# Softmax minus one-hot on one core: the middle blocks' transfers cut into four sets of every fourth partition, and the work ordered block by block

## The chip, the core and the metric

The kernel runs on one NeuronCore of one Trainium2 chip. A core has several engines that run side by side, each with its own instruction stream: VectorE (DVE in the profile), ScalarE (ACT), GpSimd (POOL), TensorE (PE) and SyncE (SP). Data moves between the device memory (HBM) and the core's on-chip memory (SBUF, 128 partitions) by DMA; the profile counts 16 DMA engines for the core. In this kernel SP and ACT issue the transfers, each into a queue of its own: the profile's q1 carries what SP issued, q10 what ACT issued.

The metric is the device time of one execution in microseconds (us). The kernel before takes 1248.91 us, the median of three runs (1248.84 to 1249.3).

## The reference

For 8 x 1024 rows of 8192 logits, the gradient of a cross entropy: the softmax of the row, less 1 at the label's column. All in fp32.

```python
logits_max = np.max(logits, axis=-1, keepdims=True)
exp_logits = np.exp(logits - logits_max)
softmax = exp_logits / np.sum(exp_logits, axis=-1, keepdims=True)
one_hot = np.zeros_like(logits)
one_hot[batch_idx, seq_idx, labels] = 1.0
return (softmax - one_hot).astype(np.float32)
```

Input and output are 268.4 MB each. Every element has to come in once and go out once.

## The kernel before

**Tiling.** The 8192 rows are cut into 32 blocks of 256 rows. In a block, partition p holds rows 2p and 2p+1 (G = 2 rows for each partition), so both in memory and in SBUF a partition's share of a block is one contiguous run of 64 KB, 32 KB for each of its two rows. A block is 8.39 MB. The big buffer `X` has three slots (SLOTS = 3); block b lives in slot b mod 3 and is computed in place: loaded, exponentiated, scaled, stored. A "row tile" t = 2b + j is one of the two rows of all 128 partitions, 128 x 8192 elements. There are 64 of them.

**Per row tile.** Four steps, each a helper of the code:

- `row_max(t)`: a VectorE reduction over the row gives the negated maximum `m`. It waits for the pieces of the load that meet this row.
- `exponentials(t)`: ScalarE's Exp in place, which also accumulates the sum `s`.
- `mark(t)`: two short ScalarE instructions on 128 x 2048 elements that write the one-hot row into PSUM (`hot`, one buffer for even and one for odd row tiles), as bytes. It may start when the row tile two before has been finished.
- `finish(t)`: on VectorE a reciprocal of `s`, and one pass X = X * r - hot in place. For the last two row tiles the pass is made in two halves of the columns.

**Transfers.** `load(b)` and `store(t)` cut a block into pieces by a letter for each block, in the strings LOADS and STORES: `r` is one transfer for each of the two rows, 128 partitions with runs of 32 KB; `s` is row by row in two sets of every second partition, 64 runs of 32 KB each, of which the second set goes by ACT's queue; `w` is the whole block in one transfer, 128 runs of 64 KB. Loads go by SP's queue, stores by ACT's. A load of block b + 3 waits for all the stores of block b that share partitions and rows with it, because it overwrites their slot. A store of a row waits for its `finish`. In the kernel before, blocks 0 to 2 are loaded as `s`, 3 and 4 as `r`, 5 to 28 as `w`, 29 to 31 as `r`, and all stores are `r`; the last block is stored in four transfers, one for each row and half of the columns.

**Order.** The string ORDER sets by a letter how the instructions of a block are put in line on VectorE and ScalarE. In the kernel before it is `r` throughout: the code interleaves, and the reduction of the next block's first row stands ahead of the finish of this block's second row. On VectorE, with t the first row tile of a block: row_max(t+1), finish(t), row_max(t+2), finish(t+1), row_max(t+3), finish(t+2) and so on. With `b` a block is done by itself: row_max(t), row_max(t+1), finish(t), finish(t+1), and only then the next block. The branch for `b` is in the code of the kernel before, unused. Stores and loads are issued from the same program order: a store of a row after its finish, the load of block b + 3 after both stores of block b.

**The helper.** All instructions go through `run`, so that in the profile nearly everything stands at its line, L76; a wait for more than one semaphore is a wait of its own at L75 ahead of the instruction. So the profile is read here by operation and by tile names.

Of the kernel before, what the change touches and what calls it, by code (L numbers as in the profile page):

```python
# [7 lines left out]
P = 128  # L8
G = 2
SLOTS = 3  # L10

LOADS = "sssrrwwwwwwwwwwwwwwwwwwwwwwwwrrr"
STORES = "rrrrrrrrrrrrrrrrrrrrrrrrrrrrrrrr"
ORDER = "rrrrrrrrrrrrrrrrrrrrrrrrrrrrrrrr"


@with_exitstack
def kernel(
# [45 lines left out]
    with tc.tile_critical():  # L64
# [6 lines left out]
        def run(engine, waits, counter, method, **operands):  # L71

            waits = list(dict.fromkeys(waits))
            for w in waits[:-1]:
                engine.wait_ge(*w)  # L75
            instruction = getattr(engine, method)(**operands)  # L76
            for w in waits[-1:]:
                instruction._wait_ge(*w)
            step = 16 if method == "dma_start" else 1
            instruction.then_inc(counter, step)  # L80
            count[counter.name] = count.get(counter.name, 0) + step
            return counter, count[counter.name]

        every, rows = slice(0, P), slice(0, G)
        one = [slice(j, j + 1) for j in range(G)]
        halves = [slice(i, P, 2) for i in range(2)]
        sides = [slice(i * V // 2, (i + 1) * V // 2) for i in range(2)]
        PIECES = {
            "r": [(every, js) for js in one],
            "s": [(ps, js) for js in one for ps in halves],  # L90
            "w": [(every, rows)],
        }

        def meets(a, b):
            sets = [[set(range(*d.indices(n))) for d, n in zip(p, (P, G))] for p in (a, b)]
            return all(x & y for x, y in zip(*sets))
# [4 lines left out]
        def load(b):  # L101
            loaded[b] = []
            before = stored.get(b - SLOTS, [])
            for q, piece in enumerate(PIECES[LOADS[b]]):
                ps, js = piece
                free = [w for other, w in before if meets(piece, other)]
                queue = nc.scalar if LOADS[b] == "s" and ps == halves[1] else nc.sync
                w = run(
# [5 lines left out]
        def store(t):  # L114
            b, j = divmod(t, G)
            stored.setdefault(b, [])
            if t >= T - G:
# [6 lines left out]
                return  # L124
            for q, piece in enumerate(PIECES[STORES[b]]):
                ps, js = piece
# [30 lines left out]
        def mark(t):  # L157
            if t >= T:
                return
            w = run(  # L160
                nc.scalar, ([made] if t < G else [freed[t - G]]) + ([marked[t - 1]] if t else []), act, "activation",
                out=away[:], in_=count16[:], func=Act.Abs, bias=at(word, t), scale=1.0,
            )
            marked[t] = run(
                nc.scalar, [w], act, "activation",
                out=hot[:, t % G, :], in_=away[:], func=Act.Relu, bias=at(unit, t), scale=at(minus, t),
            )
# [76 lines left out]
        for b in range(B):  # L244
            t0, t1 = b * G, b * G + 1
            nxt = t1 + 1
            if ORDER[b] == "b":
                if t0 not in maxed:
# [20 lines left out]
            mark(t0 + G)  # L269
            ahead = nxt < T and ORDER[b + 1] == "r"  # L270
            if ahead:
# [41 lines left out]
```

## Time and profile before

| what | value |
|---|---|
| time, median of 3 runs | 1248.91 us |
| span of the profiled execution, first to last instruction | 1246.6 us |
| VectorE busy | 1120.2 us (90%) |
| ScalarE busy | 722.7 us (58%) |
| DMA busy, mean of 16 engines, over all but the two ends | 1.00 |
| moved | 536.98 MB, mean 431 GB/s |

The profiled execution's own time was not given apart from its span; the median of the runs lies 2.3 us above the span, and what lies around the span (launch and end) is taken to be that. How to read it: a line of the page's last part and of the views by group gives the engine, the operation, output and input, and a count; "q1" and "q10" rows count the DMA packets. A packet here is one contiguous run of a transfer (a run of 32 KB or 64 KB), or the small completion message that each of the 16 engines sends at the end of a transfer.

### The profile page before, as it was taken

The numbers are of one execution on the slowest core, as the hardware profiler recorded it, in microseconds if no ns is written. First come the engines' busy times: TensorE is split into PE (matmuls) and PEld (weight loads), VectorE is DVE, ScalarE is ACT, GpSimd is POOL, SyncE is SP. The second block draws the span as 40 slices with busy tenths as digits, with TensorE's granted clock in tenths as the row PEclk, the third lists the DMA queues.
The fourth block names the chain that finished last, engine by engine and source line by source line (L and its number), as shares of the span: only waits on it lengthen the run. The fifth ranks groups of instructions, "written<-read, shape, count | busy, mean of one in ns | idle before, by whom it ended". The sixth has DMA issues, their size and how long they took to land.

```text
span 1246.6 us, 809 instructions
## 1 busy us (share of the span) xinstructions
PE 0.4 (0%) x2; PEld 0.3 (0%) x2; DVE 1120.2 (90%) x208; ACT 722.7 (58%) x257; POOL 2.3 (0%) x7
## 2 busy tenths in 40 slices
PE   0000000000000000000000000000000000000000
PEld 0000000000000000000000000000000000000000
DVE  5999998889988889888898888998889988899995
ACT  2866664556555565465655655556556555566662
POOL 0000000000000000000000000000000000000000
DMA  9999999999999999999999999999999999999998
GB/s 406 413 431 434 437 432 444 435 437 421 433 429 437 443 423 433 434 431 435 430 441 435 422 435 435 434 440 426 432 434 431 433 446 434 422 430 435 429 434 383
DMA packets 15413, 536.98 MB, mean 431 GB/s; under 512 B 1808, under 2 KB 1808, under 8 KB 1840
## 3 DMA queue, kind: packets, MB, share of 16 engines
q10 hardware_dynamic: 9744, 276.89, 51.5%
q1 hardware_dynamic: 5664, 260.05, 48.3%
q14 instruction: 5, 0.04, 0.0%
HBM read 268.50 MB, written 268.44 MB: 431 GB/s over the span
## 4 chain that ended last, share of the span: by engine, by line
DMA 59%; DVE 26%; issue 11%; ACT 3%; DVEq 0%; ACTq 0%; SPq 0%
DMA X<-in_logits_dram 33%; DMA out_dram<-X 26%; DVE X L76 15%; DVE m L76 10%; ACT X L76 2%; DVEq L64 0%; DVE r L76 0%; ACT hot L76 0%; ACT away L76 0%; ACTq L76 0%; DVEq L75 0%; ACTq L308 0%; SPq L64 0%
## 5 line engine op out<-in xcount | busy, mean ns | idle before, releaser
L76 ACT ACTIVATE X<-X,m 128x8192 f32<-128x8192 f32 x64 | 455.8, 7122 | 365.2 <-DVE m L76 365.2
L76 DVE TENSOR_REDUCE m<-X 128x1 f32<-128x8192 f32 x64 | 555.6, 8682 | 105.4 <-DMA X<-in_logits_dram 105.4
L76 DVE SCALAR_TENSOR_TENSOR X<-X,r,hot 128x8192 f32<-128x8192 f32 (+1 forms) x66 | 560.1, 8489 | 3.8 <-ACT hot L76 1.6
L76 ACT ACTIVATE away<-count,word 128x2048 bf16<-128x2048 int16 x64 | 128.1, 2001 | 127.0 <-DVE X L76 127.0
L76 ACT ACTIVATE hot<-away,unit,minus 128x2048 int32<-128x2048 bf16 x64 | 131.9, 2061 | 2.1
L76 ACT ACTIVATION_READ_ACCUMULATOR X<-X,m 128x1 f32 x64 | 11.9, 186 | 0.0
L76 DVE RECIPROCAL r<-s 128x1 f32<-128x1 f32 x64 | 9.8, 153 | 0.0
L76 ACT ACT_TABLE_LOAD x1 | 1.3, 1283 | 5.3 <-issue 5.3
L76 DVE CAST lab_f<-lab_raw 32x256 f32<-32x256 int32 x1 | 0.5, 536 | 2.7 <-DMA lab_raw<-in_labels_dram 2.7
L76 POOL IOTA count<- 128x2048 int16 x1 | 1.8, 1823 | 0.0
L76 DVE TENSOR_TENSOR unit<-unit,part 128x64 f32<-128x64 f32 x3 | 0.7, 225 | 0.1
L76 DVE CAST lab<-hot 128x64 int32<-128x64 f32 x1 | 0.2, 224 | 0.5 <-PE hot L76 0.5
L76 DVE TENSOR_SCALAR part<-minus 128x64 f32<-128x64 f32 x3 | 0.6, 194 | 0.1
L76 PE MATMUL hot<-ident,lab_f 32*128 32x32 f32 x2 | 0.4, 298 | 3.3 <-DVE lab_f L76 3.3
L76 PEld LDWEIGHTS hot<-ident,lab_f 32*128 32x128 f32 x2 | 0.3, 192 | 3.3 <-DVE lab_f L76 3.3
L76 DVE CAST minus<-lab 128x64 f32<-128x64 int32 x1 | 0.2, 195 | 0.0
L76 DVE TENSOR_SCALAR word<-part 128x64 f32<-128x64 int32 x1 | 0.2, 195 | 0.0
L76 DVE TENSOR_SCALAR lab<-lab 128x64 int32<-128x64 int32 x1 | 0.2, 195 | 0.0
L76 DVE TENSOR_SCALAR unit<-minus 128x64 f32<-128x64 f32 x1 | 0.2, 195 | 0.0
L76 DVE TENSOR_SCALAR part<-lab 128x64 int32<-128x64 int32 x1 | 0.2, 194 | 0.0
L76 DVE TENSOR_SCALAR minus<-unit 128x64 f32<-128x64 f32 x1 | 0.2, 194 | 0.0
L76 POOL TENSOR_SCALAR_AFFINE_SELECT ident<-ident 32x32 f32<-32x32 f32 x1 | 0.2, 203 | 0.1
(5 smaller groups left out, 0.5 us busy)
## 6 DMA issues: line engine op xcount, KB each, us to landing
out_dram<-X ACTq DMA_DIRECT2D x62, 4096.0 KB, 30.4
X<-in_logits_dram SPq DMA_DIRECT2D x10, 4096.0 KB, 28.1
X<-in_logits_dram SPq DMA_DIRECT2D x6, 2048.0 KB, 32.6
X<-in_logits_dram ACTq DMA_DIRECT2D x6, 2048.0 KB, 37.1
out_dram<-X SPq DMA_DIRECT2D x2, 2048.0 KB, 12.7
out_dram<-X ACTq DMA_DIRECT2D x2, 2048.0 KB, 11.9
X<-in_logits_dram SPq DMA_DIRECT2D x24, 33.4
lab_raw<-in_labels_dram ACTq DMA_DIRECT2D x1, 64.0 KB, 1.8
```

What stands on the lines that cost most here:

```text
L76: instruction = getattr(engine, method)(**operands)
```

## The change

Three strings and one new letter. The new letter `q` cuts a block into four sets of every fourth partition, each with both rows: 32 runs of 64 KB, 2.1 MB. Loads of blocks 5 to 28 become `q` where they were `w`. Stores of blocks 2 to 25 become `q` where they were `r`; since a `q` piece holds both rows, all four are issued after the finish of the block's second row. ORDER is `b` throughout. A load of block b + 3 is now cut as the store of block b is, so each of its four pieces waits for one piece of the store.

```diff
-LOADS = "sssrrwwwwwwwwwwwwwwwwwwwwwwwwrrr"
-STORES = "rrrrrrrrrrrrrrrrrrrrrrrrrrrrrrrr"
-ORDER = "rrrrrrrrrrrrrrrrrrrrrrrrrrrrrrrr"
+LOADS = "sssrrqqqqqqqqqqqqqqqqqqqqqqqqrrr"
+STORES = "rrqqqqqqqqqqqqqqqqqqqqqqqqrrrrrr"
+ORDER = "bbbbbbbbbbbbbbbbbbbbbbbbbbbbbbbb"
...
+        fourths = [slice(i, P, 4) for i in range(4)]
...
             "w": [(every, rows)],
+            "q": [(ps, rows) for ps in fourths],
         }
```

The number of transfers goes from 113 to 233: loads from 46 to 118 (24 whole blocks become 96 sets), stores from 66 to 114 (48 rows become 96 sets), and one for the labels.

## The prediction

> **What bounds the kernel now.** I read first the page's busy rows, its slices and its DMA rows.
>
> ```profile
> span 1246.6 us, 809 instructions
> PE 0.4 (0%) x2; PEld 0.3 (0%) x2; DVE 1120.2 (90%) x208; ACT 722.7 (58%) x257; POOL 2.3 (0%) x7
> DMA  9999999999999999999999999999999999999998
> DMA packets 15413, 536.98 MB, mean 431 GB/s; under 512 B 1808, under 2 KB 1808, under 8 KB 1840
> q10 hardware_dynamic: 9744, 276.89, 51.5%
> q1 hardware_dynamic: 5664, 260.05, 48.3%
> ```
>
> VectorE at 90% looks like the bound at first. But the two DMA queues together hold 51.5 + 48.3 = 99.8% of all the time of 16 engines. So I read the waits and a stretch of the chain next, and then the stages by window.
>
> ```profile
> DVE m L76 <- DMA X<-in_logits_dram: 105.4, 26, 8.9
> ...
> 637.14 26.24 DMA out_dram<-X
> 663.38 0.02 issue
> 663.40 33.30 DMA X<-in_logits_dram
> ```
>
> ```profile
> core 0: us, PE busy (x) PEld busy (x) DVE busy (x) ACT busy (x) POOL busy (x), PEclk, DMA share, GB/s
> 10.00:50.00 40.00, 0.00 (x0) 0.00 (x0) 31.66 (x5) 25.40 (x10) 0.00 (x0) 1.00 1.00 433
> 50.00:62.00 12.00, 0.00 (x0) 0.00 (x0) 11.96 (x4) 8.14 (x3) 0.00 (x0) 1.00 1.00 399
> 165.00:1080.00 915.00, 0.00 (x0) 0.00 (x0) 821.48 (x142) 530.10 (x189) 0.00 (x0) 1.00 1.00 433
> 1080.00:1200.00 120.00, 0.00 (x0) 0.00 (x0) 116.13 (x22) 74.01 (x27) 0.00 (x0) 1.00 0.99 428
> ```
>
> VectorE's waits for data (105.4 us in 26) are the larger part of its idle time. The chain shows why: a store of 26 us, a load of 33 us in the slot that it freed, then compute. That looks like a chain of latencies, which finer pieces would shorten. The windows say that it isn't: from 10 us on the DMA share is 1.00 at 433 GB/s, in the middle as at the start. The store and the load last long because they share full engines. Shortening a wait then only moves the same bytes in another order. The bound is bytes over 16 engines, plus what each packet costs beside its bytes.
>
> So the questions are three: does the change alter what the packets cost, does it leave the engines without work anywhere, and does a set of 32 partitions move as fast as 128.
>
> **The packets.** Three short windows show what one packet takes; in each row stand packets, MB and the share of 16 engines. The first holds one completion message, the second row tiles' stores alone, the third has loads of whole blocks on q1.
>
> ```profile
> DMA packets 1, 0.00 MB, mean 0 GB/s; under 512 B 1, under 2 KB 1, under 8 KB 1
> q10 hardware_dynamic: 1, 0.00, 0.6%
> ...
> DMA packets 256, 7.34 MB, mean 432 GB/s; under 512 B 32, under 2 KB 32, under 8 KB 32
> q10 hardware_dynamic: 256, 7.34, 100.0%
> ...
> DMA packets 138, 6.09 MB, mean 435 GB/s; under 512 B 16, under 2 KB 16, under 8 KB 16
> q1 hardware_dynamic: 64, 4.19, 69.1%
> ```
>
> The first window is 0.1 us long (1244.9 to 1245): 0.6% of 16 x 0.1 us is 0.0096 us for a message. The second is 17 us long (1202 to 1219): 272.0 us of engine time, less 32 messages (0.31 us), over 224 runs of 32 KB gives 1.2129 us each. The third is 14 us long (638 to 652): 69.1% of 224 us over 64 runs of 64 KB (4.19 MB over 64 is 65.5 KB, so q1 holds no message there) gives 2.4185 us. Two runs of 32 KB take 2.4258 us, so joining them saves 0.0073 us. With the shares' rounding (0.05% each) that is 0.004 to 0.010 us.
>
> *Removed.* Loads of blocks 5 to 28 are in runs of 64 KB already and stay so; "transfers of 64 KB runs" is new for the stores alone. There 24 blocks x 128 partitions = 3072 pairs of runs become one, 192 on each engine: 192 x 0.0073 = 1.40 us (0.8 to 2.0).
>
> *Added.* 1808 small packets are 16 for each of 113 transfers; 233 transfers have 3728. That is 1920 more, 120 on each engine: 120 x 0.0096 = 1.15 us if each takes the engine for itself, 0 if it hides beside a run of the other queue. I take 1.15, since the row shows that time.
>
> *Bytes*: the same. So the DMA's work changes by 1.15 - 1.40 = -0.25 us, between -2.0 and +0.35.
>
> **Issuing, and the engines.**
>
> ```profile
> L76 ACTq DMA_DIRECT2D out_dram<-X x64: 337/338/373, 44.6 to 1233.1; - x64
> L76 SPq DMA_DIRECT2D X<-in_logits_dram x40: 327/328/657, 1.0 to 1173.0; - x40
> L76 ACT ACTIVATE X<-X,m 128x8192 f32<-128x8192 f32 x64 | 455.8, 7122 | 365.2 <-DVE m L76 365.2
> L76 ACT ACTIVATE hot<-away,unit,minus 128x2048 int32<-128x2048 bf16 x64 | 131.9, 2061 | 2.1
> L76 ACT ACTIVATE away<-count,word 128x2048 bf16<-128x2048 int16 x64 | 128.1, 2001 | 127.0 <-DVE X L76 127.0
> 1101.76 8.68 DVE L76 TENSOR_REDUCE m<-X 128x1 f32<-128x8192 f32 x1
> 1110.36 0.15 DVE L76 RECIPROCAL r<-s 128x1 f32<-128x1 f32 x1
> 1110.54 8.75 DVE L76 SCALAR_TENSOR_TENSOR X<-X,r,hot 128x8192 f32<-128x8192 f32 x1
> 1119.21 8.68 DVE L76 TENSOR_REDUCE m<-X 128x1 f32<-128x8192 f32 x1
> ```
>
> VectorE needs 1119.21 - 1101.76 = 17.45 us for a row tile, 34.9 for a block. The DMA needs 2 x 8.39 MB / 433 GB/s = 38.75 us. In the new order, finish(t) stands behind row_max(t+1) (8.68 us), and the Exp that it needs takes 7.12 + 0.19: hidden. The second Exp hides behind finish(t) (8.75). On ScalarE four issues of 0.34 (1.35 us, before 0.68) and a mark (2.0 + 2.06) come after the block's last finish, 5.4 us in all; the next Exp can start only after the next block's first reduction, 8.68 us later. So the added issues are behind that, at nothing; without this cover 0.68 us of ScalarE a block, still below the slack of 3.85 us that VectorE has. Of the waits that the change moves, the four stores on ACT's queue wait for the block's second finish, and behind them stand that mark and the next Exp, for which VectorE asks last; on SP's queue a set waits for its own store, and behind it stands only the next set, whose store ends later. SP has nothing else to do but issue, 96 x 0.33 us. VectorE's extra waits, six a block, are for semaphores that have come by then or come with the last piece; the row shows gaps of a few hundredths of a us between instructions, so 0.3 us a block at most, in the same slack.
>
> **Do the engines run dry?** A middle block's store now starts when its second row is finished: for the first row 8.9 us later. Take the moment a block b is finished: its slot has 8.39 MB to store, and 8.39 MB of load queue behind it set by set. That is 38.75 us of DMA work, and VectorE hands over the next block 34.9 us later at the earliest. If instead VectorE stands still for data, a load is in flight by definition. So the middle stays full. A set's load waits for its store to land, but three other sets (4.8 us each at full rate) are in the ring meanwhile.
>
> The first place at risk is block 2, the first stored in sets. From the timeline's start of the first reduction at 15.75 us the new order finishes block 0 at 56 us, block 1 at 91 and block 2 at about 126 (44.5 us for the first finish, then from 47.1, when the second Exp is done, one pass, and two blocks of 34.9). Until then five loads and two stored blocks, 58.7 MB, can move; at the 423 GB/s of the first 155 us they last 139 us. A margin of 12 us.
>
> ```profile
> 15.75 8.69 DVE L76 TENSOR_REDUCE m<-X 128x1 f32<-128x8192 f32 x1 [8.91 <-DMA X<-in_logits_dram]
> 35.78 8.75 DVE L76 SCALAR_TENSOR_TENSOR X<-X,r,hot 128x8192 f32<-128x8192 f32 x1 [1.56 <-ACT hot L76]
> 39.74 7.11 ACT L76 ACTIVATE X<-X,m 128x8192 f32<-128x8192 f32 x1
> 0.00:155.00 155.00, 0.41 (x2) 0.28 (x2) 139.63 (x37) 95.27 (x35) 2.31 (x7) 1.00 0.99 423
> ```
>
> At the end, the window from 1202 has no q1 packet: stores alone for the last 43 us. When the last load lands, at most a reduction and two finishes are left on VectorE (8.68 + 2 x 8.9 = 26.5 us) and a last store of 11.9 us to landing (below); 38.4 in all, against two whole blocks to store, 38.75 us. Covered, by the old margin or little less.
>
> ```profile
> out_dram<-X ACTq DMA_DIRECT2D x2, 2048.0 KB, 11.9
> lab_raw<-in_labels_dram ACTq DMA_DIRECT2D x1, 64.0 KB, 1.8
> ```
>
> **Sum.** 1246.6 - 0.25 = 1246.35 us of span, and the 2.3 us by which the median stands above it: 1248.6 us. Own range 1246.9 to 1249.3. VectorE will wait less or elsewhere, and that is worth nothing.
>
> **Rivals.**
>
> *The hand-over hole (slower).* A set's load starts only when its set is stored, and a store lands some time after its last byte; the label's small load took 1.8 us in all. If the other ring is empty at that moment, once a block, 24 x 1.8 = 43 us are lost: 1292. It decides as soon as less than 1.8 us of work stands in the rings. For it: all stores of a block start together, so the two rings can fall into step. Against: 38.75 against 34.9 us. 10%.
>
> *The sets move slower (slower).* Two runs for each engine instead of eight may not spread as evenly, and the page has no set of 32 partitions. The nearest rows are the sets of 64 at the start, 433 GB/s between 10 and 50 us, which is no loss, and, as the other end, 428 between 1080 and 1200: 402.7 MB in sets at 428 instead of 433 is 10.9 us, 1259.5. 5%.
>
> *A fixed price for each transfer (slower).* 120 transfers more, each with the label's 1.8 us on the path, is 216 us: 1465. Against it: stores alone keep the engines at 100.0% over 17 us in which two transfers ended (32 messages). 3%. [...]
>
> *Faster.* The fixed cost of a run at its upper bound (2.0 us), messages for nothing, and the slow stretch at 50 to 62 us (399 instead of 433 GB/s, 0.94 us) gone: 1246.6 - 2.94 + 2.3 = 1246.0. Against: the stretch belongs to blocks 0 to 2, cut as before. 5%.
>
> **How the numbers follow.** The forecast holds 77%, all of it within 0.2% (2.5 us, what a measurement can tell from no change here). Faster 5%, slower 10 + 5 + 3 = 18%. The range starts at 1246.5, below the forecast's lower bound, and reaches to 1254, half of the second rival, which leaves out 2 in 10.
>
> **What would show it.** Small packets 3728 and some 10,500 runs; queue shares that still sum to 99.8%; 433 or 434 GB/s in the middle; chain pieces that name other transfers while the span stays. Wrong would be: slices of DMA under 9 after the start (the hole), a full share at fewer GB/s (slower sets), or VectorE without waits for loads (then it, not the DMA, is the bound).

## The result, and the profile after

The changed kernel takes 1252.2 us, the median of 5 runs (1251.07 to 1255.52); the kernel before, on the same chip, takes 1248.84 (1248.18 to 1249.3). The ratio is 1.0034, with the 95% interval from 1.0021 to 1.0047: it is 3.4 us slower. The profiled execution took 1254.47 us, of which the span is 1252.7; it is one of the longer ones, so what its trace shows is more than the 3.4 us of the medians. Medians below are of all runs and ratios of the undisturbed ones alone, and for two experiments only a median is left.

The page of the changed kernel, the rows that answer to those of before:

```profile
span 1252.7 us, 1001 instructions
PE 0.4 (0%) x2; PEld 0.3 (0%) x2; DVE 1120.3 (89%) x208; ACT 722.8 (58%) x257; POOL 2.3 (0%) x7
DMA  9999999999999999999999999999999999999997
DMA packets 14264, 537.02 MB, mean 429 GB/s; under 512 B 3728, under 2 KB 3728, under 8 KB 3760
q10 hardware_dynamic: 7440, 276.90, 51.3%
q1 hardware_dynamic: 6816, 260.05, 48.3%
```

The engines compute as long as before, and no slice before the last has lost its 9. The small packets are the 3728 that were counted ahead. The two queues together hold 99.6% instead of 99.8% of the 16 engines' time, at 429 GB/s instead of 431. So there is a little more idle time, and the busy time moves less.

VectorE's wait for loads, and a stretch of the chain that ended last (start, duration, what):

```profile
DVE m L76 <- DMA X<-in_logits_dram: 104.3, 27, 9.0
```

```profile
626.80 45.29 DMA out_dram<-X
672.11 33.56 DMA X<-in_logits_dram
705.83 8.47 issue
714.30 7.40 DVE m L76
```

VectorE still stands 104 us for data (105.4 before). The chain names longer pieces, a store of 45 us where it was 26, and yet in that part of the program nothing is lost: these lengths are queueing in front of full engines (a share of 1.00 at 434 GB/s from 345 to 1070 us, below). Where the loss is, only the rate by stretches of time shows. First the windows of the kernel before (window, length, busy time of each engine, clock, DMA share, GB/s), then those of the changed one. A run is counted whole in the window in which it begins, so a short window can show a share above 1.00; its rate divided by its share is then the rate of full engines:

```profile
10.00:137.00 127.00, 0.00 (x0) 0.00 (x0) 118.48 (x20) 82.71 (x30) 0.00 (x0) 1.00 1.00 430
137.00:152.00 15.00, 0.00 (x0) 0.00 (x0) 14.96 (x4) 9.49 (x4) 0.00 (x0) 1.00 1.04 448
152.00:345.00 193.00, 0.00 (x0) 0.00 (x0) 171.71 (x30) 111.32 (x40) 0.00 (x0) 1.00 1.00 433
345.00:1070.00 725.00, 0.00 (x0) 0.00 (x0) 652.77 (x112) 420.51 (x150) 0.00 (x0) 1.00 1.00 434
1070.00:1105.00 35.00, 0.00 (x0) 0.00 (x0) 31.30 (x7) 21.14 (x8) 0.00 (x0) 1.00 0.98 421
1105.00:1235.00 130.00, 0.00 (x0) 0.00 (x0) 127.81 (x25) 76.29 (x27) 0.00 (x0) 1.00 1.00 432
1240.00:1245.00 5.00, 0.00 (x0) 0.00 (x0) 0.00 (x0) 0.00 (x0) 0.00 (x0) 1.00 0.68 292
1245.00:1250.00 5.00, 0.00 (x0) 0.00 (x0) 0.00 (x0) 0.00 (x0) 0.00 (x0) 1.00 0.00 2
```

```profile
10.00:137.00 127.00, 0.00 (x0) 0.00 (x0) 115.90 (x20) 78.01 (x29) 0.00 (x0) 1.00 1.00 429
137.00:152.00 15.00, 0.00 (x0) 0.00 (x0) 14.93 (x4) 11.93 (x5) 0.00 (x0) 1.00 1.01 415
152.00:345.00 193.00, 0.00 (x0) 0.00 (x0) 174.49 (x30) 112.78 (x41) 0.00 (x0) 1.00 1.00 430
345.00:1070.00 725.00, 0.00 (x0) 0.00 (x0) 653.49 (x111) 421.33 (x150) 0.00 (x0) 1.00 1.00 434
1070.00:1105.00 35.00, 0.00 (x0) 0.00 (x0) 34.93 (x7) 22.55 (x8) 0.00 (x0) 1.00 0.99 416
1105.00:1235.00 130.00, 0.00 (x0) 0.00 (x0) 123.48 (x25) 74.88 (x26) 0.00 (x0) 1.00 1.00 431
1240.00:1245.00 5.00, 0.00 (x0) 0.00 (x0) 0.00 (x0) 0.00 (x0) 0.00 (x0) 1.00 0.93 397
1245.00:1250.00 5.00, 0.00 (x0) 0.00 (x0) 0.00 (x0) 0.00 (x0) 0.00 (x0) 1.00 0.37 157
```

Three things stand there.

- From 345 to 1070 us both kernels move 434 GB/s. A steady state of sets costs neither more nor less than one of whole loads and row stores.
- From 137 to 345 us and again from 1070 to 1105 the changed kernel moves less at a full share. These are the changes from rows to sets and back, called passages here: block 2, the first stored as a set, is finished at 126 us, and at 1070 to 1105 the cuts go back to rows. Rate over share gives 448 / 1.04 = 431 before and 415 / 1.01 = 411 after from 137 to 152 us, and 430 and 420 from 1070 to 1105. The rates' differences times the windows' lengths give, from 10 to 1235 us, 0.13 + 0.50 + 0.58 + 0 + 0.18 + 0.13 = 1.5 MB, which is 3.5 us at 433 GB/s (the rounding of the long window alone is worth over 1 us). The records of the single runs agree: a run of 32 KB nearly always takes 1.213 us and one of 64 KB 2.418, and what the runs took above that adds up, for each engine, to about 5.6 us in the changed kernel and 2.5 in the one before. From 137 to 345 us it is 2.6 against 0.1, from 1070 to 1105 1.1 against 0.0, and between these two 0.1 against 0.8. A run that took longer than usual is called a stretched run from here on.
- After 1240 us the engines have 0.93 x 5 + 0.37 x 5 = 6.5 us of work each, where they had 3.4. That is the 3.1 us again. But it is spread unevenly: between 1245 and 1250 more and more engines are idle while some still work. Of the 6.1 us by which the profiled span grew, about 3.1 are stretched runs and the rest is this spread. The last engine ends this kernel, not the mean of 16: from 1245 to 1250 us that mean is 0.37.

The changed kernel's first passage, 137 to 152 us, read out (all packets, then the load queue's: packets, MB, share of 16 engines):

```profile
DMA packets 149, 6.23 MB, mean 415 GB/s; under 512 B 20, under 2 KB 20, under 8 KB 20
q1 hardware_dynamic: 68, 2.23, 39.0%
```

The 68 load packets are runs of 32 KB (2.23 MB over 68), of blocks that are still loaded by rows of 128 partitions. They take 39.0% of 240 us over 68 = 1.38 us each instead of 1.21. So at a passage it isn't the runs of the sets alone that are stretched.

### The profile page after: what moved, and what is told of

It reads as the page before. It is cut to its first block, busy times and chain, and to the rows that moved or that the text cites. A ratio compares the mean times of both kernels' runs of the same rounds, so it can differ in the third digit from the quotient of the medians.

```text
span 1252.7 us, 1001 instructions
## 1 busy us (share of the span) xinstructions
PE 0.4 (0%) x2; PEld 0.3 (0%) x2; DVE 1120.3 (89%) x208; ACT 722.8 (58%) x257; POOL 2.3 (0%) x7
## 2 busy tenths in 40 slices
DMA packets 14264, 537.02 MB, mean 429 GB/s; under 512 B 3728, under 2 KB 3728, under 8 KB 3760
## 4 chain that ended last, share of the span: by engine, by line
DMA 57%; DVE 25%; issue 11%; ACT 2%; another core or an unknown queue 2%; ACTq 1%; DVEq 0%; SPq 0%
DMA out_dram<-X 33%; DMA X<-in_logits_dram 25%; DVE X L76 14%; DVE m L76 11%; ACTq L76 1%; ACT X L76 1%; DVE r L76 0%; DVEq L64 0%; ACT hot L76 0%; ACT away L76 0%; DVEq L75 0%; SPq L76 0%; ACTq L310 0%; ACTq L75 0%
## 5 line engine op out<-in xcount | busy, mean ns | idle before, releaser
L76 DVE TENSOR_REDUCE m<-X 128x1 f32<-128x8192 f32 x64 | 553.1, 8680 | 104.3 <-DMA X<-in_logits_dram 104.3
```

## Experiments

All diffs are against the changed kernel, and `b` order is kept unless the diff says otherwise. The kernel before took 1248.25 to 1248.58 us on the same chips. The letters of theories hold within one group of runs; the text beside a letter says what it holds.

### The order alone, and the cut alone

```diff
 e1_order_only
-LOADS = "sssrrqqqqqqqqqqqqqqqqqqqqqqqqrrr"
-STORES = "rrqqqqqqqqqqqqqqqqqqqqqqqqrrrrrr"
+LOADS = "sssrrwwwwwwwwwwwwwwwwwwwwwwwwrrr"
+STORES = "rrrrrrrrrrrrrrrrrrrrrrrrrrrrrrrr"
 e2_sets_only
-ORDER = "bbbbbbbbbbbbbbbbbbbbbbbbbbbbbbbb"
+ORDER = "rrrrrrrrrrrrrrrrrrrrrrrrrrrrrrrr"
```

> Only ORDER is b; the transfers are cut as before. Theory S (the sets of 32 partitions put the 16 engines out of step and slow runs where the cut changes): 1248.8 us, ratio 0.999 to 1.001, the last store's 16 completions within 3 us of each other as before. Rival O (the order by block costs it): 1251.5 to 1253. Rival L (runs of 64 KB in both directions at once cost it): 1248.8, as S.

> The middle blocks in sets of every fourth partition both ways, ORDER r as before. Theory S: 1251.5 to 1253, ratio about 1.003, engines 7 us or so apart at the end. Rival O: 1248.8. Rival L: 1251.5 to 1253, as S.

Measured: the order alone 1248.58 us, ratio 1.0001 [0.9992, 1.0009]; the sets in the old order 1270.37, 1.0166 [1.0143, 1.0190]. The order costs nothing by itself, and with the sets it saves 18 us; that was in none of the forecasts for the second run. Without it the stretched runs are 25.9 us an engine, 22.9 of them in the 64 KB loads, and they go on through the whole middle, where the load queue runs empty 62 times (in the changed kernel once between 165 and 1070 us; gaps of over 0.3 us without a load run are counted).

### Other cuts in both directions

```diff
 e3_whole_both
+LOADS = "sssrrwwwwwwwwwwwwwwwwwwwwwwwwrrr"
+STORES = "rrwwwwwwwwwwwwwwwwwwwwwwwwrrrrrr"
 e4_halves_both
+LOADS = "sssrrhhhhhhhhhhhhhhhhhhhhhhhhrrr"
+STORES = "rrhhhhhhhhhhhhhhhhhhhhhhhhrrrrrr"
+            "h": [(ps, rows) for ps in halves],
 e9_rows_both
+LOADS = "sssrrrrrrrrrrrrrrrrrrrrrrrrrrrrr"
+STORES = "rrrrrrrrrrrrrrrrrrrrrrrrrrrrrrrr"
```

> Middle blocks move whole both ways, one transfer of 128 runs of 64 KB each way, ORDER b: the runs of the changed kernel without its sets. Theory S: 1247 to 1249 us, no slower than before, engines within 3 us at the end. Rival L: 1251.5 to 1253, as the changed kernel. Rival O: 1251.5 to 1253.

> Middle blocks in two sets of every second partition, both rows, runs of 64 KB, ORDER b: four runs for each engine in a transfer instead of two (sets) or eight (whole). Theory S with the number of runs for each engine as its cause: between, 1249 to 1251. Rival L: 1251.5 to 1253.

> All middle blocks row by row both ways, runs of 32 KB only, ORDER b. Theory L: no slow runs; 1248.8 us plus 192 runs more for each engine at 0.0073 us (1.4), so 1250. If mixing run lengths is what keeps before undisturbed: slower than 1252.

Measured: whole blocks 1290.59 us, 1.0323 [1.0297, 1.0348]; two sets of every second partition 1258.82, 1.0081 [1.0049, 1.0113]; rows 1248.57, 1.0001 [0.9992, 1.0010]. The first two lie outside every forecast.

The slices of the page of the kernel with whole blocks, and its window over the middle and over one hole, show what the prediction called the hand-over hole:

```profile
DMA  9999999999989999999999999999999999999998
```

```profile
165.00:1070.00 905.00, 0.00 (x0) 0.00 (x0) 774.16 (x134) 498.13 (x178) 0.00 (x0) 1.00 0.98 413
358.00:361.00 3.00, 0.00 (x0) 0.00 (x0) 2.71 (x1) 0.00 (x0) 0.00 (x0) 1.00 0.05 22
```

The load of a slot must wait for the whole block's store there, and the engines run out of work: one slice in the middle falls below 9, and the share of 0.98 over 905 us is 18 us of holes. In the hole at 358 to 361 us the share is 0.05 at 22 GB/s, the work of about one engine of 16. But the loss is 42 us. The rest is again at a full share: runs are stretched, many of them right after such a hole, by 29.6 us an engine in all. So this isn't a matter of sets of 32 partitions alone; whole transfers of 128 have it too.

Rows in both directions leave all runs at 32 KB, and the time is that of before. This bears on the other half of the prediction's sum, the prices of joined runs and of messages. The same window, 400 to 1000 us, of the kernel before, of the changed one and of rows both ways:

```profile
DMA packets 6658, 259.65 MB, mean 433 GB/s; under 512 B 736, under 2 KB 736, under 8 KB 736
```

```profile
DMA packets 5956, 260.09 MB, mean 433 GB/s; under 512 B 1984, under 2 KB 1984, under 8 KB 1984
```

```profile
DMA packets 8926, 259.91 MB, mean 433 GB/s; under 512 B 992, under 2 KB 992, under 8 KB 992
```

From 3972 to 7934 runs, and from 736 to 1984 messages, move the same within 0.44 MB, 1 us of 600. The prices forecast for this window are smaller than that (about 0.4 us saved and 0.75 us added for an engine, by the prediction's 0.0073 and 0.0096 us), so these windows neither confirm nor refute them. They do show that the two prices aren't the loss.

### Sets in one direction alone

```diff
 e6_stores_sets
+LOADS = "sssrrwwwwwwwwwwwwwwwwwwwwwwwwrrr"
 e7_loads_sets
+STORES = "rrrrrrrrrrrrrrrrrrrrrrrrrrrrrrrr"
 e10_set_rows
+STORES = "rrpppppppppppppppppppppppprrrrrr"
+            "p": [(ps, js) for js in one for ps in fourths],
 (and eight semaphores for each slot instead of four)
 e16_halves_loads
+LOADS = "sssrrhhhhhhhhhhhhhhhhhhhhhhhhrrr"
+STORES = "rrrrrrrrrrrrrrrrrrrrrrrrrrrrrrrr"
```

> Loads whole as before, stores of the middle blocks in sets of every fourth partition with runs of 64 KB, ORDER b. Theory L (runs of 64 KB in both directions at once slow some runs, loads above all): slower, 1251 to 1290 us, slow load runs in the middle. Theory S (sets of 32 partitions): 1250 to 1252. If sets soften what whole transfers do, it lies between the changed kernel (1252) and the whole both ways (1290).

> Loads of the middle blocks in sets with runs of 64 KB, stores row by row with runs of 32 KB, ORDER b. Theory L: 1248 to 1249.5 us, the middle without slow runs as before. Theory S: 1250.5 to 1253.

> The changed kernel with its middle stores cut once more, by row: eight sets of 32 runs of 32 KB instead of four of 64 KB; loads in sets of 64 KB runs, ORDER b. Theory L: no slow runs, 1249.5 to 1251 us (1.4 for the runs, 0.9 for 96 completion messages more on each engine), engines together at the end. Theory S: 1252 to 1254, engines 7 us apart at the end.

> Loads in two sets of every second partition with runs of 64 KB (four runs for each engine in a transfer), stores by rows, ORDER b: between whole loads beside stores by rows (1248.6, eight runs) and loads in four sets beside them (1280.7, two runs). If the few runs of a set for each engine cost at each restart of the load queue: 1255 to 1270. If every cut into sets does: 1275 to 1285.

Measured: sets for stores alone 1298.1 us, 1.0397 [1.0382, 1.0413]; sets for loads alone 1280.73, 1.0255 [1.0235, 1.0275]; loads in sets with stores in eight sets of 32 KB runs 1278.33, 1.0242 [1.0225, 1.0259]; halves for loads alone 1252.61, 1.0036 [1.0023, 1.0049]. So sets of every fourth partition in one direction cost 32 to 50 us, in both with the stores cut by rows as well 30, and in both, cut alike, 3.4. For halves it is the other way round: 4 us in loads alone, which is below both forecasts, and 10 in both. Theory L is refuted, since the loads in sets lose as much beside 32 KB stores; theory S has the sign, but its sizes are far too small. With sets for stores alone a whole load has to wait for all four sets of its slot, and the window from 165 to 1070 us shows a share of 0.99 at 413 GB/s: small holes and stretched runs, as with whole blocks.

The kernel with sets for loads alone shows stretched runs at their plainest. At 243.5 us its load queue starts again after 7 us of stores alone. Its window from 243 to 250 us (packets and MB, then q1's packets, MB and share of 16 engines):

```profile
DMA packets 51, 2.72 MB, mean 389 GB/s; under 512 B 0, under 2 KB 0, under 8 KB 0
q1 hardware_dynamic: 32, 2.10, 79.2%
```

And the order alone, from 241 to 248 us, where the load queue starts again with a whole block after 10 us of stores alone:

```profile
DMA packets 61, 3.05 MB, mean 435 GB/s; under 512 B 0, under 2 KB 0, under 8 KB 0
q1 hardware_dynamic: 32, 2.10, 69.4%
```

Both hold 32 load runs of 64 KB, two for each engine. They take 79.2% of 112 us over 32 = 2.77 us each in the first and 2.43 in the second, and the stores beside them move less as well: 0.33 MB lost in 7 us, 0.8 us. This comes back with every block, 0.9 us on the mean; with the order alone the same restart costs 0.05 us on the mean, with halves 0.05.

### Sets from the first block to the last, and 32 neighbours

```diff
 e5_sets_throughout
+LOADS = "qqqqqqqqqqqqqqqqqqqqqqqqqqqqqqqq"
+STORES = "qqqqqqqqqqqqqqqqqqqqqqqqqqqqqqqr"
 e8_quarters
+LOADS = "kkkkkkkkkkkkkkkkkkkkkkkkkkkkkkkk"
+STORES = "kkkkkkkkkkkkkkkkkkkkkkkkkkkkkkkr"
+            "k": [(slice(32 * i, 32 * i + 32), rows) for i in range(4)],
```

> All blocks in sets both ways from the first load on (only the last block's stores stay cut by rows), ORDER b: no change of cut at 126 us and at 1075 us. Theory R (a set's runs are slow when its queue starts again after running empty, because 16 engines start in step and collide until they have drifted apart; once apart they stay so while the queue never empties): slow runs in the first load-only stretch, few later; 1248 to 1252 us. Theory C (the changes of cut are what costs): 1247.5 to 1249.

> As the sets throughout, but a set is a quarter of 32 neighbouring partitions instead of every fourth. [...] If only the size of the transfer and the restart decide: within 1% of the sets throughout.

Measured: sets throughout 1261.76 us, 1.0099 [1.0074, 1.0125], slower than either theory had it; 32 neighbouring partitions 1682.55 us. Windows of the first:

```profile
55.00:66.00 11.00, 0.00 (x0) 0.00 (x0) 11.00 (x2) 3.37 (x2) 0.00 (x0) 1.00 0.67 286
165.00:1070.00 905.00, 0.00 (x0) 0.00 (x0) 821.83 (x141) 529.68 (x188) 0.00 (x0) 1.00 1.00 433
1245.00:1255.00 10.00, 0.00 (x0) 0.00 (x0) 0.00 (x0) 0.00 (x0) 0.00 (x0) 1.00 0.74 318
```

With no passage in the middle, it is at the full rate again. It pays at its ends: a hole of 0.33 x 11 = 3.6 us around the first stores, and engines that end apart. So doing away with passages by cutting everything into sets is no way out.

How the 32 partitions are chosen matters more than anything else here. In the window from 10 to 50 us there are loads almost alone. First every fourth partition, then neighbours:

```profile
DMA packets 400, 17.83 MB, mean 446 GB/s; under 512 B 128, under 2 KB 128, under 8 KB 128
q1 hardware_dynamic: 400, 17.83, 102.9%
```

```profile
DMA packets 224, 8.42 MB, mean 211 GB/s; under 512 B 80, under 2 KB 80, under 8 KB 96
q1 hardware_dynamic: 192, 8.39, 101.6%
```

The second moves 128 runs of 64 KB in 101.6% of 640 us: 5.1 us each against 2.42. So the loads of 32 neighbours move at half the rate, 211 GB/s, where every fourth partition takes the full rate (446 at a share of 1.029). Stores pay less: by the page of the kernel with neighbours, q10 moves 264.31 MB in 39.9% of 16 engines' span of 1687.7 us, 2.67 us for each 64 KB. The size of the transfer and the restart alone would have left the time within 1% of the sets throughout; it is 33% longer. What makes neighbours slow is not shown.

### What keeps the changed kernel near 1252: each set waits only for its own piece

```diff
 e12_drain
-                free = [w for other, w in before if meets(piece, other)]
+                free = [w for _, w in before]
```

> The changed kernel with one thing undone: each of the four load sets waits for all four store sets of its slot instead of for its own, so that the load queue runs empty once a block; cuts and order stay. Theory R: slow load runs once a block, 1262 to 1295 us, as the order r with sets (1270) and sets in one direction alone (1281, 1298). Theory M (unlike cuts of the two directions, or the order r, were what cost there): 1251 to 1255, as the changed kernel.

The edit holds for every load of a block whose slot has been stored, the loads by rows included.

Measured: 1305.46 us, 1.0484 [1.0428, 1.0540], more than theory R had. Its window over the middle:

```profile
165.00:1070.00 905.00, 0.00 (x0) 0.00 (x0) 771.67 (x133) 500.19 (x178) 0.00 (x0) 1.00 0.98 411
```

Share 0.98 instead of 1.00 is 18 us of holes, and the stretched runs of the whole program are 35 us an engine. The 53 us above the changed kernel are what the waits by pieces are worth.

### The passages counted: twelve blocks in sets, in one, two and four stretches

```diff
 e13_one_change
+LOADS = "sssrrqqqqqqqqqqqqrrrrrrrrrrrrrrr"
+STORES = "rrqqqqqqqqqqqqrrrrrrrrrrrrrrrrrr"
 e14_two_changes
+LOADS = "sssrrqqqqqqrrrrrrqqqqqqrrrrrrrrr"
+STORES = "rrqqqqqqrrrrrrqqqqqqrrrrrrrrrrrr"
 e15_four_changes
+LOADS = "sssrrqqqrrrqqqrrrqqqrrrqqqrrrrrr"
+STORES = "rrqqqrrrqqqrrrqqqrrrqqqrrrrrrrrr"
```

> The changed kernel with half as many blocks in sets: 12 blocks in sets, then rows both ways, ORDER b; one stretch of sets as in the changed kernel. Theory C (what is lost is lost at the passages between rows and sets, one into the stretch and one out of it): 1251.5 to 1253 us, as the changed kernel. Theory P (lost evenly over the blocks in sets): 1250 to 1250.8, half the loss.

> The same 12 blocks in sets, in two stretches of six with six blocks in rows between them. Theory C: twice the loss of one stretch, 1255 to 1257 us. Theory P: as with one stretch, 1250 to 1250.8.

> The same 12 blocks in sets, in four stretches of three. Theory C: four times the loss, 1260 to 1265 us. Theory P: 1250 to 1250.8.

Measured: one stretch 1253.49 us, 1.0063 [1.0038, 1.0089]; two 1292.59 (single runs from 1268.54 to 1303.99); four 1305.02, 1.0459 [1.0432, 1.0486]. Half the blocks in sets, in one stretch, cost as much as all of them, and half of them in four stretches cost 57 us. So the loss doesn't go by the number of blocks, which refutes theory P. It grows with the number of passages, but with two and four stretches it is about six and four times what theory C had. The windows of the kernel with one stretch, whose sets end near 600 us, show it:

```profile
125.00:175.00 50.00, 0.00 (x0) 0.00 (x0) 49.93 (x9) 32.29 (x11) 0.00 (x0) 1.00 1.02 434
175.00:590.00 415.00, 0.00 (x0) 0.00 (x0) 374.38 (x66) 242.44 (x88) 0.00 (x0) 1.00 1.00 433
590.00:640.00 50.00, 0.00 (x0) 0.00 (x0) 49.68 (x10) 31.93 (x11) 0.00 (x0) 1.00 0.99 414
640.00:1070.00 430.00, 0.00 (x0) 0.00 (x0) 393.13 (x69) 255.15 (x91) 0.00 (x0) 1.00 1.00 433
```

The passage back, which was at 1070 us, has moved to 590 to 640: 414 instead of 433 GB/s over 50 us, about 2 us. On both sides of it the rate is full. In the first stretch the load queue stands empty for about 1 us at every set, at no cost: from 175 to 590 us the share is 1.00 at 433 GB/s all the same. With two and four stretches the rate doesn't stay full any more. Of the kernel with two, its second stretch of sets and the rows behind it; then, of the kernel with four, the two long windows:

```profile
600.00:900.00 300.00, 0.00 (x0) 0.00 (x0) 227.00 (x40) 144.23 (x54) 0.00 (x0) 1.00 0.94 391
920.00:1200.00 280.00, 0.00 (x0) 0.00 (x0) 260.02 (x44) 166.01 (x60) 0.00 (x0) 1.00 1.00 431
```

```profile
175.00:590.00 415.00, 0.00 (x0) 0.00 (x0) 370.62 (x66) 238.40 (x86) 0.00 (x0) 1.00 1.00 419
640.00:1070.00 430.00, 0.00 (x0) 0.00 (x0) 351.70 (x61) 221.10 (x79) 0.00 (x0) 1.00 0.96 401
```

The price of a passage isn't fixed. After a later one the runs stay stretched and holes come (shares 0.94 and 0.96) for as long as the stretch of sets lasts, and they end with the return to rows. Why the one long stretch keeps the full rate and a later one doesn't is not shown.

### Why the runs are stretched: addresses, bytes of a run, or runs for each engine

```diff
 e17_sets_in_line, e18_loads_in_line
+        def place(letter, q, ps):
+            return slice(32 * q, 32 * q + 32) if letter == "q" else ps
...
-                    out=X[ps, b % SLOTS, js, :], in_=x_b[b, ps, js, :],
+                    out=X[ps, b % SLOTS, js, :], in_=x_b[b, place(LOADS[b], q, ps), js, :],
...
-                    out=o_b[b, ps, js, :], in_=X[ps, b % SLOTS, js, :],
+                    out=o_b[b, place(STORES[b], q, ps), js, :], in_=X[ps, b % SLOTS, js, :],
 e18_loads_in_line also
+STORES = "rrrrrrrrrrrrrrrrrrrrrrrrrrrrrrrr"
 e19_loads_row_sets, without place
+LOADS = "sssrrpppppppppppppppppppppppprrr"
+STORES = "rrrrrrrrrrrrrrrrrrrrrrrrrrrrrrrr"
+            "p": [(ps, js) for js in one for ps in fourths],
 (and eight semaphores for each slot instead of four)
```

> The changed kernel, but set k of a block lies in memory as the k-th quarter of the block in one piece (2.1 MB in line) instead of as every fourth 64 KB of it; in SBUF it is every fourth partition as before. The output's rows of blocks loaded or stored otherwise stand in other places, and the one-hot subtracts at another row's label. Theory A (the addresses: strided 64 KB pieces in memory are what slows the runs at the passages): 1247.5 to 1249.5, as before the change. Theory P (only the SBUF side and the few runs of a transfer matter, the addresses in memory don't): 1251 to 1256, as the changed kernel, slow runs again near 140 and 1080 us.

> Load sets against row stores (which took 1280.7 us), with the load sets' memory in line as in the run before; rows go out at other places than they came from. Here the load queue runs empty and restarts all the time, so the price of a restart shows at its largest. Theory A: most of the 32 us goes, below 1260. Theory P: 1274 to 1286, no change.

> Load sets against row stores again, but each set is cut by rows too: eight transfers a block, 32 runs of 32 KB each, two for each engine. Theory N (the price hangs on the number of runs that each engine gets from one transfer, two): 1275 to 1290, as with 64 KB runs. Theory B (it hangs on the bytes of a run, so that 32 KB runs escape it as the row transfers' do): under 1260. Theory T (each transfer that follows an empty queue costs a fixed time, so twice the transfers cost more): over 1295.

Measured: sets that lie in line in memory 1255.69 us, 1.0061 [1.0035, 1.0087]; the same for loads alone 1277.65, 1.0249 [1.0196, 1.0303], where 1280.73 was without; row sets for loads alone 1302.72, 1.0426 [1.0409, 1.0444]. The addresses in memory aren't the cause. Nor is a run's length: with runs of 32 KB, still two for each engine in a transfer, the loss is larger. The time lies in the range of theory T, but the loss, 54 us against 32, isn't double, as a fixed price for each transfer would have it, and it stands in other places: the load runs are 25.6 us above their usual time (23.3 with 64 KB runs), the stores 16.7 (5.7), and the engines end further apart. Nor does the load queue run empty more often here, 26 times against 41 in the middle, so these runs aren't stretched by restarts alone. The window of this kernel's end:

```profile
1270.00:1305.00 35.00, 0.00 (x0) 0.00 (x0) 26.57 (x7) 10.52 (x4) 0.00 (x0) 1.00 0.61 257
```

What stretches a run at a restart or a passage stays open. What the runs rule out as the cause are the addresses and the length of a run; that it is a matter of the 32 partitions alone is ruled out by the whole blocks and by the row loads at the changed kernel's first passage. That it hangs on how evenly the 16 engines are staggered when they start is the author's guess and not shown: which engine moves which partitions isn't in the records, and no run varied that by itself. No cut that was tried is faster than the kernel before; the order alone and rows both ways equal it.

## Why the prediction was wrong

- **The bound.** Right. DMA work sets the time, with the two queues at 99.6% of the 16 engines' time; VectorE's waits and the chain's names moved about without effect.
- **The packets.** The counts were right: 3728 messages, and 14264 - 3760 - 8 = 10,496 long runs where some 10,500 were forecast. The prices hold in the steady state, as far as the windows of 600 us can tell: -0.25 us was "nothing", and no difference shows. *This is the step that failed, though*: it took a run's duration from windows in the steady state (1.2129 and 2.4185 us) and used it for every run of the program, so it put the passages between cuts at nothing. At the passages a run takes more, on the mean 1.38 instead of 1.21 us in the one that was read out above, and the term that was missing is about 3.1 us an engine in the profiled execution.
- **A row that could have warned.** The trace of before has such a passage: from 50 to 62 us, where the loads in sets end and the stores begin, it moves 399 GB/s at a share of 1.00. The prediction read this as a slow stretch worth 0.94 us, used it only for the rival "faster", and didn't ask whether new changes of cut would bring more of the same. The records give 0.9 us of stretched runs there, before and after the change.
- **One pool of 16 engines.** The sum took the mean share of 16 engines for the end of the program. In the changed kernel the engines end further apart, which put about another 3 us on the profiled span. That the stretched runs drive them apart is argued, not shown, since the records don't name the engine. This term had no row in the trace of before; a restart of the load queue had one, and costs 0.03 us there.
- **Issuing and the engines.** Right: VectorE waits 104.3 us for loads, and block 2 is finished at 126 us as worked out; neither there nor behind the last load does a window's share show a hole.
- **Do the engines run dry.** Right, at 1.00 through the middle. That each set waits only for its own store is needed for it, as the run that took this away shows: 53 us.
- **The rivals.** "The sets move slower" came nearest, full engines that move less, but had the wrong place, and its ground ("two runs for each engine instead of eight may not spread as evenly") is not shown: it was priced as 1% on all bytes in sets (10.9 us), while the steady state moves 434 GB/s and the passages pay. The hand-over hole did not come, but it did in the experiments with whole blocks and without waits by pieces (0.98 over the middle in both). The fixed price for each transfer is refuted by the middle, 434 GB/s before and after. "Faster" had its ground in the price of a run, which the windows don't resolve.
- **The size around the span.** The profiled executions lie 1.8 us above their span, where 2.3 was taken. It changes nothing in the sign.
- **Range and chances.** The 77% for no change stood on the steady state alone, and the time lies 0.9 us beyond the 2.5 us that this allowed. The prediction names two ranges: the sum's own, 1246.9 to 1249.3, is missed by 2.9 us; the wider one, 1246.5 to 1254, holds the time, by luck, since its upper part was there for a loss in the steady state.

## What to carry to other kernels

When the DMA engines are full, a new cut of the transfers is not judged by its steady state alone: here it moved 434 GB/s before and after, and the kernel was 3.4 us slower. Count the passages between cuts and the places where a queue starts again, and read the GB/s there in windows of 10 to 50 us at a full share. If blocks go in sets of every fourth partition, cut loads and stores alike: 1252.2 us here, against 1280.73 and 1298.1 with sets in one direction alone (whole loads beside stores by rows cost nothing, 1248.58 us, and halves were better in one direction alone, 1252.61 against 1258.82). Let each piece of a load wait for its own piece of a store, which was worth 53 us, and change the cut as seldom as possible: 12 blocks in sets cost 5 us in one stretch and 57 in four. And at the end look at how far apart the 16 engines finish: the last of them ended the changed kernel, and the spread is about 3 us of its profiled span.

## What the runs showed of the hardware that was not expected

- DMA engines that were busy all the time moved 10% less: 389 GB/s over 7 us after a load queue of sets started again, against 435 with whole transfers of 128 partitions. The share of busy time doesn't show this (100.5% and 100.8% over the two queues), only the rate does.
- Twelve blocks in sets cost 5 us in one stretch (1253.49 us) and 57 in four (1305.02).
- Sets of 32 neighbouring partitions load at 211 GB/s (share 1.016), sets of every fourth one at 446 (1.029), both over the 40 us from 10 to 50.
- Runs of 32 KB and of 64 KB, and 2.7 times as many completion messages, move the same 433 GB/s from 400 to 1000 us.
